# Moving the products of GpSimd to VectorE in a planned decoder kernel, with the modulation let go earlier and the planner's numbers set anew

## The chip, the cores and the metric

The kernel runs on one core of one Trainium2 chip. The metric is the device time of one launch in microseconds, as the median of several runs. A profiled execution gives the trace from which the rows below come.

## The reference, cut to what matters

A decoder trunk of two layers works on 512 tokens of width 1024, all in float32. Each layer has a mixing half and a channel half:

```python
for layer in range(DEPTH):
    mod = einsum('bd,de->be', silu(c), w_mod[layer]) + b_mod[layer]   # 6 vectors of 1024
    shift1, scale1, gate1, shift2, scale2, gate2 = split(mod, 6)
    h = rms_norm(x, mix_norm_w[layer]) * (1 + scale1) + shift1
    proj = h @ w_in[layer]                  # one product for three mixers
    y_a = deltanet_mixer(...)               # gated delta rule: conv, decay, chunks, scan
    y_b = spatial_gating_mixer(...)         # gMLP: layer norm of v, causal 128x128 mixing, gate u
    y_c = dilated_attention_mixer(...)      # three windows, merged by their denominators
    x = x + gate1 * (concat([y_a, y_b, y_c]) @ w_out[layer])
    h = rms_norm(x, ffn_norm_w[layer]) * (1 + scale2) + shift2
    gate, up = split(h @ w_ffn_in[layer], 2)
    x = x + gate2 * ((silu(gate) * up) @ w_ffn_out[layer])
```

In the gated delta rule a triangular decay matrix E is built for each chunk and masked to its causal half. In the spatial gating the mixing matrix `w_s` is masked to its causal half, and v is normalised, multiplied by `ln_g` and shifted by `ln_b`.

## The kernel before, in words

Activations lie transposed, 128 channels on the partitions and 512 tokens along the free axis. A large product is computed in three matmuls: every operand is split into a rounded part `hi` (ScalarE copies) and the rest `lo` (VectorE subtracts), and `mm3` (L581) multiplies hi by hi, hi by lo and lo by hi. One PSUM bank holds a tile of 128 by 512.

**Weights** come as pieces of 512 KB. `loader` (L454) issues their DMAs on the queue of SyncE into a ring of four `raw` buffers, in a fixed order. A buffer is free again when `splitter` (L497) has made hi and lo of it, or, for the modulation's pieces, when `modulation` (L478) has used it. `modulation` forms each of the 96 columns of `mod` with one VectorE instruction over a piece of 128 by 1024. In layer 0 the columns come in the order 0, 8, 1, 9, 2, 10, and so on: a shift, then the scale of the same chunk of 128 channels. Chunks 1 to 7 wait for the flag `go`, which the first chunk of the normalised input sets when its work has been emitted (L1463).

**The order of the work** is not written by hand. Each part of the layer is a generator, a task. `Plan` (L87) keeps estimated times of the engines, of each tile and of the DMA queue. Its `run` (L221) resumes, among the tasks that could go on, the one with the lowest priority number, and what that task emits is appended to the instruction streams of the engines. So the planner's estimates and the ranks (`PR0` for layer 0, `PR1` for layer 1) set the order in which each engine gets its instructions, and an engine runs them strictly in that order. `yield V` means: go on when VectorE's estimated queue is nearly empty. For a DMA the planner estimates the landing from a bandwidth of 423 GB/s (L177).

**The parts that the change touches.** `decay` (L801) makes one matrix E of 128 by 512 for each of four token blocks: two VectorE products with a triangle (`gts`), two matmuls with `slowr`, an exponential on ScalarE, and a product with the triangle on GpSimd (L817). `triangle` (L820) then needs E. `gmlp` (L1096) multiplies `ws` (128 by 512) by the triangle on GpSimd (L1104) and normalises v: for each of four blocks one VectorE instruction, then one GpSimd product and one GpSimd sum of 128 by 256 (L1121, L1122). Matmuls of v with `ws` follow. GpSimd also does the memsets: 24 of 64 by 512 for the attention's keys (L1219) and a few small ones.

**The tails.** At the end of a layer's projections the flag `h_done` lets the outputs of the mixers be split (`dn_out`, `gated`, `merge`), and the output projection takes them in `Y_ORDER`. `attention` (L1279) runs eight blocks for each of its two parts, at most three at a time.

Of the kernel before, what the change touches and what calls it, by code (L numbers as in the profile page):

```python
# [13 lines left out]
ALU = mybir.AluOpType  # L14
# [3 lines left out]
P = 128  # L18
T = 512
D = 1024  # L20
NB = T // P
KC = D // P
NH = 4
# [23 lines left out]
M_FIRST = 0  # L47


PR0 = dict(norm0=1, norm1=0.2, res=1.2, swin=5, val=0.2, hid=0, attn=2.5, inv=2, scan=0.4, norm=2, out=0.6, qk0=6.5,  # L50
           qk1=5, qk2=4, att0=3.5, att1=0.6, merge=2.5, gm=1.8, kd=0.1, o=1.8, tables=0.1, conv=0.2, convv=1.8, E=1,
           B=0, blocks=0.2, kss=1.2, gates=5, scales=1, tri=2.2, yb=1, qss=2.5, vv=1, split=0.2, mod=0.4)
PR1 = dict(norm0=5, norm1=2.2, res=0.1, swin=0.2, val=0.2, hid=3, attn=4, inv=1.2, scan=2.5, norm=1, out=1.2,
           qk0=2.5, qk1=4, qk2=6.5, att0=2, att1=1, merge=0.2, gm=1, kd=0.8, o=2, tables=3, conv=0.8, convv=2, E=0.1,
           B=1.5, blocks=1.8, kss=0.2, gates=6.5, scales=3.5, tri=0.1, yb=5, qss=1.8, vv=0.1, split=5, mod=0.1)
PRS = PR0, PR1
LOOSE = dict(o2=5, f1=16, t=8)
SPARE = dict(tile=1, tiles=1, n=0, out=1)
# [10 lines left out]
              qk0=[("n", i) for i in range(4)], qk1=[("n", i) for i in range(4, 8)], qk2=[("n", i) for i in range(8, 12)],  # L69
# [17 lines left out]
class Plan:  # L87
# [76 lines left out]
    def note(self, eng, op, args, kw):  # L164
        aps = [a for a in list(args) + list(kw.values()) if isinstance(a, bass.AP)]
        outs = [kw["out"] if "out" in kw else args[0]]
        if "accum_out" in kw:
            outs.append(kw["accum_out"])
        ins = [a for a in aps if not any(a is o for o in outs)]
        start = max([self.busy["Q" if eng == "D" else eng], self.now if eng == "D" else 0.0]  # L170
                    + [self.when(a, eng) for a in ins] + [self.when(o, eng) for o in outs if eng != "PE"]
                    + [self.read(o, eng) for o in outs])
        if eng == "D":
            start = max(start, self.landed[self.count % 8])
            self.busy["Q"] = start + 0.47
            scratch = any(a.space == bass.MemoryType.DRAM and "scr" in a.tensor.name for a in ins + outs)
            end = max(start + (2.2 if self.count not in (2, 3) else 3.1), self.busy["D"] + (0.9 if self.count in (2, 3) else 0)) + 4 * math.prod(outs[0].shape) / (120e3 if scratch else 423e3)  # L177
            self.busy["D"] = self.landed[self.count % 8] = end
            self.count += 1
        else:  # L180
            if eng == "S":
                self.func = args[2]
            kw = dict(kw, scalar=args[2]) if op == "scalar_tensor_tensor" else kw
            two = len([a for a in ins if a.space != PSUM]) > 1
            if eng == "V" and two and start < self.port[1] and start + 0.3 > self.port[0]:
                start = self.port[1]
            elif eng == "G" and two:
                start = max(start, min(self.busy["V"], start + 1.2))
            end = start + self.cost(eng, op, outs, ins, kw, start)
            self.busy[eng] = end  # L190
            if eng == "G" and two:
                self.port = start, end
            end += self.TAIL[eng]
        for a in ins:
            last = self.last.setdefault(a.tensor.name, {})
            last[eng] = max(last.get(eng, 0.0), end)
        for o in outs:
            name, lo, hi = self.span(o)
            w = self.wrote.setdefault(name, [])
            w[:] = [x for x in w if x[0] < lo or x[1] > hi] + [(lo, hi, end, eng)]  # L200
# [103 lines left out]
def _trunk(ctx, tc, xT, cb, consts, prm, gmp, wmod, wt, wn, wab, wo, wo2, wf1, wf2, out):  # L304
# [3 lines left out]
    PE, V, S, G, Q = plan.engines  # L308
# [41 lines left out]
    def b3(ap, n):  # L350
        return ap.rearrange("p (a b) -> p a b", a=n)
# [5 lines left out]
    def every(ap, n, w):  # L357

        return ap.rearrange("p (o j) -> p o j", o=1).to_broadcast([P, n, w])
# [28 lines left out]
    triu = cst[:, C_TRIU:C_TRIU + 128]  # L388
# [55 lines left out]
    rings, hold, go, go_lo, late = {}, [0], Flag(), Flag(), Flag()  # L444
# [33 lines left out]
    def modulation():  # L478

        soon = lambda: plan.busy["V"] - M_SLACK  # L480
        todo = [p[0] for p in pieces if p[0][0] == "mod"]
        while todo:
            _, l, j = todo.pop(0)
            near = V if l or j >= 16 else soon
            if l or j >= 16:
                mod_task.prio = PR0["mod"]
            if not l and 0 < j < 8:
                yield go
            yield near, lambda: plan.ready(raws[1][0][0]) if raws[1] and not hold[0] else None
            raw, got = raws[1].pop(0)  # L490
            bias = prs[l][:, L_BMOD + j:L_BMOD + j + 1]
            V.tensor_tensor_reduce(out=raw, in0=raw, in1=cact, op0=ALU.mult, op1=ALU.add,
                                   scale=1.0, scalar=bias, accum_out=mods[l][:, j:j + 1])
            mod_ok[l, j].done = True
            got.done = True
# [305 lines left out]
    def decay(c, g):  # L801

        yield arena.need(7)
        gts = [slot(F32R) for _ in range(2)]
        E = slot()
        for gt, gp in zip(gts, g):
            V.tensor_tensor(b3(gt, NH), every(triu, NH, P), heads(gp[:, 4 * c:4 * c + 4].bitcast(F32), NH, P), op=ALU.mult)
        yield parts_ok, tuple(gts)
        ps = yield from bank()
        PE.matmul(ps, slowr, gts[0], start=True, stop=False)  # L810
        PE.matmul(ps, slowr, gts[1], start=False, stop=True)
        free(*gts)
        yield S, ps
        S.activation(E, ps, AF.Exp)
        bankf(ps)
        yield E
        G.tensor_tensor(b3(E, NH), b3(E, NH), every(triu, NH, P), op=ALU.mult)  # L817
        return E

    def triangle(c, kT, s1, E, bc4):  # L820
# [7 lines left out]
        yield V, ps, E  # L828
        B, = yield from slots(1)
        for h in range(NH):  # L830
# [265 lines left out]
    def gmlp(l, vg):  # L1096

        ws, ln = yield from slots(2, 4)
# [2 lines left out]
        Q.dma_start(out=ln, in_=gmp[l, :, 512:1024])  # L1101
        Q.dma_start(out=bs, in_=gmp[l, :, 1024:1280])
        yield cst_ok, late, ws
        G.tensor_tensor(b3(ws, 4), b3(ws, 4), every(triu, 4, P), op=ALU.mult)  # L1104
        yield vg
        vg = vg.value
        yield V, tuple(vg)
# [9 lines left out]
        for b in range(NB):  # L1117
            yield V
            t = vg[b // 2][:, 256 * (b % 2):256 * (b % 2) + 256]
            V.tensor_scalar(t, t, mv[:, 2 * b:2 * b + 1], r[:, b:b + 1], op0=ALU.subtract, op1=ALU.mult)  # L1120
            G.tensor_tensor(t, t, ln[:, 0:256], op=ALU.mult)  # L1121
            G.tensor_tensor(t, t, ln[:, 256:512], op=ALU.add)  # L1122
        free(ln)
        yield tuple(vg)
        ts = []
        for hp in range(2):
            ps = yield from bank()
            for b in range(NB):
                for e in range(2):
# [3 lines left out]
                              start=True, stop=True)  # L1133
            yield V, ps
            t, = yield from slots(1, 4)
# [229 lines left out]
    res = lambda b: slice(b, T, 4)  # L1365
# [556 lines left out]
```

## Time and profile before

| what | value |
|---|---|
| median of 3 runs | 1485.01 us (1483.36 to 1487.52) |
| profiled execution | 1488.29 us |
| its span, first to last instruction | 1486.5 us |
| TensorE matmul busy | 1445.4 us, 97% |
| TensorE weight load busy | 1231.7 us, 83% |
| VectorE busy | 911.7 us, 61% |
| ScalarE busy | 593.0 us, 40% |
| GpSimd busy | 48.0 us, 3% |
| HBM | 119 GB/s over the span |
| mean granted TensorE clock | 0.993 |

A busy share is an average over stages: the same engine may be full in one stretch and idle in the next. Idle time in front of an engine's instruction carries the name of what ended it, as in `[2.41 <-DVE w]`: VectorE, which wrote a tile w, released it. PE is TensorE's matmul, PEld its weight load, DVE VectorE, ACT ScalarE, POOL GpSimd, SP SyncE. The program's helper (L255) records every operation, so all rows have that line, and groups are told apart by tiles and shapes.

### The profile page before, as it was taken

How to read it: one execution, taken by the hardware profiler on the slowest of the kernel's cores; microseconds unless marked ns; L12 is line 12 of the kernel's file. 1: busy time of each engine (PE TensorE's matmuls, PEld its weight loads, DVE VectorE, ACT ScalarE, POOL GpSimd, SP SyncE). 2: the span in 40 equal slices, each digit the busy share in tenths (PEclk: the TensorE clock that was granted, in tenths of full speed). 3: DMA queues.
4: the chain of work that ended last, by engine and by line, in shares of the span. 5: the costliest groups of instructions: out<-in, count | busy, mean ns of one | idle time of the engine just before them, and what ended most of it. 6: DMA issues, size and time to landing. Idle time of an engine off the chain costs nothing. (4 is left out here: it accounts for less than half of the span.)

```text
span 1486.5 us, 19674 instructions
## 1 busy us (share of the span) xinstructions
PE 1445.4 (97%) x7644; PEld 1231.7 (83%) x7644; DVE 911.7 (61%) x1870; ACT 593.0 (40%) x1048; POOL 48.0 (3%) x61
## 2 busy tenths in 40 slices
PE   7899999999999999999999899999999999999998
PEld 5687988887988888888898789988789888888887
DVE  6799996937765555555487888656476333333332
ACT  4494326564432212222346532468444222122221
POOL 0022000000000000000000300100000000000000
PEclk9999999999999999999999999999999999999999
DMA  8723462503166566656333133021141222222231
GB/s 289 248 89 105 120 208 71 164 20 116 59 214 195 187 199 196 195 187 198 93 103 94 45 105 86 29 85 36 38 156 43 99 98 90 96 99 99 99 105 52
DMA packets 70637, 178.89 MB, mean 120 GB/s; under 512 B 25104, under 2 KB 25744, under 8 KB 70544
## 3 DMA queue, kind: packets, MB, share of 16 engines
q1 hardware_dynamic: 70544, 177.64, 37.8%
q8 instruction: 60, 0.98, 0.3%
q14 instruction: 33, 0.27, 0.1%
HBM read 174.40 MB, written 3.21 MB: 119 GB/s over the span
## 5 line engine op out<-in xcount | busy, mean ns | idle before, releaser
L255 PE MATMUL b<-w,hi 128*128 128x512 f32 (+1 forms) x2748 | 844.2, 389 | 12.3 <-ACT w L255 8.6
L255 PEld LDWEIGHTS b<-w,hi 128*128 128x128 f32 x2748 | 510.8, 188 | 119.9 <-ACT w L255 11.4
L255 PE MATMUL b<-w,lo 128*128 128x512 f32 (+1 forms) x1374 | 530.6, 387 | 1.0 <-DVE lo L255 1.0
L255 ACT ACTIVATE hi<-raw 128x1024 fp32r<-128x1024 f32 (+2 forms) x215 | 222.2, 1035 | 521.0 <-PE b L255 315.8
L255 DVE TENSOR_TENSOR lo<-raw,hi 128x1024 fp32r<-128x1024 f32 (+2 forms) x215 | 256.3, 1194 | 238.4 <-ACT hi L255 237.5
L255 PEld LDWEIGHTS b<-w,lo 128*128 128x128 f32 x1374 | 258.7, 188 | 54.1 <-DVE lo L255 1.8
L255 PE MATMUL b<-w,w 128*128 128x256 f32 (+2 forms) x1808 | 219.7, 287 | 3.4 <-DVE w L255 1.6
L255 PEld LDWEIGHTS b<-w,w 128*128 128x128 f32 (+1 forms) x1808 | 204.0, 185 | 20.3 <-ACT w L255 8.6
L255 PE MATMUL b<-hi,w 128*128 128x512 f32 (+2 forms) x768 | 211.7, 363 | 0.7 <-DVE w L255 0.7
L255 ACT ACTIVATE w<-b 128x512 f32<-128x512 f32 (+1 forms) x205 | 109.2, 558 | 191.3 <-PE b L255 190.1
L255 PEld LDWEIGHTS b<-hi,w 128*128 128x128 f32 x768 | 145.4, 210 | 14.8 <-DVE w L255 1.0
L255 PE MATMUL b<-lo,w 128*128 128x512 f32 (+2 forms) x384 | 137.0, 357 | 0.0
L255 DVE CUSTOM_DVE_ANT_0 raw<-raw,cact,pr 128x1024 f32<-128x1024 f32 x96 | 122.8, 1284 | 2.4 <-DMA raw<-in_wmod_dram 2.4
L255 ACT ACTIVATE w<-w 128x512 f32<-128x512 f32 (+3 forms) x204 | 103.3, 527 | 42.1 <-DVE w L255 41.2
L255 DVE TENSOR_TENSOR w<-w,b 128x512 f32<-128x512 f32 x68 | 46.3, 686 | 109.4 <-PE b L255 108.3
L255 DVE TENSOR_TENSOR w<-w,w 128x512 fp32r<-128x512 f32 (+2 forms) x119 | 79.0, 671 | 46.8 <-ACT w L255 45.6
L255 PEld LDWEIGHTS b<-lo,w 128*128 128x128 f32 x384 | 80.4, 209 | 7.8
L255 DVE SCALAR_TENSOR_TENSOR xs<-b,mod,xs 128x512 f32<-128x512 f32 (+1 forms) x56 | 37.1, 671 | 57.1 <-PE b L255 57.0
L255 PE MATMUL b<-cst,w 128*128 128x128 f32 (+1 forms) x392 | 55.6, 273 | 3.2 <-DVE w L255 3.2
L255 PEld LDWEIGHTS b<-cst,w 128*128 128x128 f32 x392 | 46.5, 146 | 10.5 <-DVE w L255 3.8
L255 DVE SCALAR_TENSOR_TENSOR w<-w,cw,w 128x511 f32<-128x511 f32 (+2 forms) x72 | 51.9, 761 | 2.7 <-ACT w L255 2.3
L255 ACT ACTIVATE w<-w,mod 128x256 fp32r<-128x256 f32 (+1 forms) x56 | 29.8, 539 | 51.6 <-DVE w L255 51.6
(93 smaller groups left out, 659.0 us busy)
## 6 DMA issues: line engine op xcount, KB each, us to landing
raw<-in_wf_dram SPq DMA_DIRECT2D x132, 512.0 KB, 4.0
raw<-in_wmod_dram SPq DMA_DIRECT2D x96, 512.0 KB, 3.6
raw<-in_wt_dram SPq DMA_DIRECT2D x36, 512.0 KB, 3.6
raw<-in_wn_dram SPq DMA_DIRECT2D x36, 512.0 KB, 3.6
raw<-in_wo_dram SPq DMA_DIRECT2D x16, 320.0 KB, 2.9
raw<-in_wo_dram SPq DMA_DIRECT2D x6, 512.0 KB, 3.2
raw<-in_wab_dram SPq DMA_DIRECT2D x4, 544.0 KB, 5.7
xs<-in_xT_dram SPq DMA_DIRECT2D x8, 256.0 KB, 5.2
```

What stands on the lines that cost most here:

```text
L255: r = f(*args, **kw)
```

## The change

GpSimd's product of E with the triangle, its product of `ws` with the triangle, and its products and sums of the layer norm are issued on VectorE instead. The wait for `go` is left out of `modulation`. The planner estimates a DMA's landing with 350 GB/s instead of 423 from the sixteenth on. All ranks that the two tables hold may have other values. No array, no matmul and no DMA is added or left out.

```diff
-PR0 = dict(norm0=1, norm1=0.2, res=1.2, swin=5, val=0.2, hid=0, attn=2.5, inv=2, scan=0.4, norm=2, out=0.6, qk0=6.5,
-           qk1=5, qk2=4, att0=3.5, att1=0.6, merge=2.5, gm=1.8, kd=0.1, o=1.8, tables=0.1, conv=0.2, convv=1.8, E=1,
-           B=0, blocks=0.2, kss=1.2, gates=5, scales=1, tri=2.2, yb=1, qss=2.5, vv=1, split=0.2, mod=0.4)
-PR1 = dict(norm0=5, norm1=2.2, res=0.1, swin=0.2, val=0.2, hid=3, attn=4, inv=1.2, scan=2.5, norm=1, out=1.2,
-           qk0=2.5, qk1=4, qk2=6.5, att0=2, att1=1, merge=0.2, gm=1, kd=0.8, o=2, tables=3, conv=0.8, convv=2, E=0.1,
-           B=1.5, blocks=1.8, kss=0.2, gates=6.5, scales=3.5, tri=0.1, yb=5, qss=1.8, vv=0.1, split=5, mod=0.1)
+PR0 = dict(norm0=2.2, norm1=5, res=2.5, swin=2.2, val=1.2, hid=0.4, attn=2.5, inv=0.1, scan=1.8, norm=1.8, out=3.5,
+           qk0=6.5, qk1=3, qk2=4, att0=3.5, att1=0.6, merge=4, gm=2.2, kd=5, o=0.1, tables=2, conv=0.2, convv=4,
+           E=1.2, B=0, blocks=0.2, kss=1.2, gates=0.2, scales=1.5, tri=1.2, yb=4, qss=2.5, vv=6.5, split=0.2, mod=0.4)
+PR1 = dict(norm0=1, norm1=3.5, res=2, swin=3, val=0.2, hid=1, attn=4, inv=6.5, scan=2.5, norm=0.1, out=2.2, qk0=2.5,
+           qk1=3, qk2=6.5, att0=2, att1=2.2, merge=0.2, gm=4, kd=6.5, o=1.8, tables=0.2, conv=1.2, convv=2, E=0.6,
+           B=4, blocks=1.8, kss=2.5, gates=0.1, scales=0.6, tri=0.6, yb=3, qss=1.8, vv=0.1, split=2, mod=0.2)
...
-            end = max(...) + 4 * math.prod(outs[0].shape) / (120e3 if scratch else 423e3)
+            end = max(...) + 4 * math.prod(outs[0].shape) / (120e3 if scratch else 423e3 if self.count < 15 else 350e3)
...
-            if not l and 0 < j < 8:
-                yield go
...
-        yield E
-        G.tensor_tensor(b3(E, NH), b3(E, NH), every(triu, NH, P), op=ALU.mult)
+        yield V, E
+        V.tensor_tensor(b3(E, NH), b3(E, NH), every(triu, NH, P), op=ALU.mult)
...
-        G.tensor_tensor(b3(ws, 4), b3(ws, 4), every(triu, 4, P), op=ALU.mult)
+        yield V
+        V.tensor_tensor(b3(ws, 4), b3(ws, 4), every(triu, 4, P), op=ALU.mult)
...
-            G.tensor_tensor(t, t, ln[:, 0:256], op=ALU.mult)
-            G.tensor_tensor(t, t, ln[:, 256:512], op=ALU.add)
+            V.tensor_tensor(t, t, ln[:, 0:256], op=ALU.mult)
+            V.tensor_tensor(t, t, ln[:, 256:512], op=ALU.add)
```

## Rows read from the trace of the kernel before

**Rows 1.** The page, busy time: engine, busy us, share of the span, instructions.
```profile
PE 1445.4 (97%) x7644; PEld 1231.7 (83%) x7644; DVE 911.7 (61%) x1870; ACT 593.0 (40%) x1048; POOL 48.0 (3%) x61
```

**Rows 2.** Waits of TensorE: releaser, us in total, times, longest us.
```profile
PE b L255 <- DVE w L255: 17.1, 19, 2.8
```

**Rows 3.** Stretches: busy us (instructions) of each engine, granted clock, DMA share, GB/s.
```profile
15.00:20.00 5.00, 3.88 (x18) 2.62 (x17) 4.05 (x16) 2.29 (x3) 0.00 (x0) 1.00 0.59 193
...
60.00:65.00 5.00, 3.47 (x8) 2.48 (x8) 5.00 (x10) 2.07 (x3) 1.31 (x1) 0.50 0.80 279
...
105.00:110.00 5.00, 2.80 (x12) 1.96 (x14) 5.00 (x7) 4.94 (x7) 2.65 (x2) 0.72 0.37 107
...
130.00:135.00 5.00, 4.64 (x24) 4.36 (x25) 5.00 (x17) 4.50 (x15) 0.00 (x0) 0.66 0.24 90
```

**Rows 4.** GpSimd's groups: shapes, count, busy us, mean ns, idle before and releaser.
```profile
L255 POOL TENSOR_TENSOR w<-w,cst 128x512 f32<-128x512 f32 x10 | 18.0, 1816 | 519.6 <-DVE w L255 449.3 <-DMA cst<-in_consts_dram 58.6 <-ACT w L255 11.7
L255 POOL TENSOR_TENSOR w<-w,w 128x256 f32<-128x256 f32 x16 | 15.6, 992 | 105.2 <-DVE w L255 104.6
```

**Rows 5.** VectorE in order of time, layer 0: start us, us, operation, idle before.
```profile
60.10 1.75 DVE L255 SCALAR_TENSOR_TENSOR w<-w,mod,w 128x512 fp32r<-128x512 f32 x1
...
101.57 1.23 DVE L255 SCALAR_TENSOR_TENSOR w<-w,cw,w 128x511 f32<-128x511 f32 x1
...
107.07 1.21 DVE L255 SCALAR_TENSOR_TENSOR w<-w,cw,w 128x510 f32<-128x510 f32 x1
...
114.47 4.90 DVE L255 TENSOR_TENSOR w<-cst,s 128x512 fp32r<-128x512 f32 x8
...
120.63 1.07 DVE L255 TENSOR_SCALAR s<-s 128x16 int32<-128x16 int32 x1
...
124.24 1.65 DVE L255 TENSOR_SCALAR s<-s 128x16 f32<-128x16 f32 x1
125.93 0.17 DVE L255 TENSOR_TENSOR s<-s,s 128x16 f32<-128x16 f32 x1
```

**Rows 6.** VectorE in layer 1, in order of time.
```profile
828.30 8.67 DVE L255 TENSOR_TENSOR w<-cst,s 128x512 fp32r<-128x512 f32 x8
```

**Rows 7.** TensorE's instructions that waited, in order of time.
```profile
59.59 0.79 PE L255 MATMUL b<-w,hi 128*128 128x512 f32 x1 [2.73 <-ACT w L255]
61.91 0.79 PE L255 MATMUL b<-w,hi 128*128 128x512 f32 x1 [1.53 <-DVE w L255]
...
107.20 0.79 PE L255 MATMUL b<-w,band 128*128 128x512 f32 x1 [2.41 <-DVE w L255]
...
130.35 1.43 PE L255 MATMUL b<-w 128*128 128x128 f32 x8 [2.75 <-DVE w L255]
...
827.21 0.81 PE L255 MATMUL b<-s,cst 128*128 128x16 f32 x6 [1.41 <-DVE s L255]
...
835.82 0.50 PE L255 MATMUL b<-w,slowr 128*128 128x512 f32 x1 [1.11 <-DVE w L255]
```

**Rows 8.** VectorE's groups by shape: count, busy us, mean ns.
```profile
L255 DVE CUSTOM_DVE_ANT_0 raw<-raw,cact,pr 128x1024 f32<-128x1024 f32 x96 | 122.8, 1284 | 2.4 <-DMA raw<-in_wmod_dram 2.4
...
L255 DVE SCALAR_TENSOR_TENSOR w<-w,cw,w 128x509 f32<-128x509 f32 x24 | 17.7, 746 | 0.1
...
L255 DVE TENSOR_TENSOR w<-w,w 128x256 f32<-128x256 f32 x16 | 6.8, 423 | 3.0 <-ACT w L255 2.4
...
L255 DVE TENSOR_TENSOR w<-w,cst 128x512 f32<-128x512 f32 x8 | 5.5, 682 | 0.0
```

**Rows 9.** TensorE at the layers' tails, in order of time.
```profile
340.20 0.49 PE L255 MATMUL b<-w,hi 128*128 128x512 f32 x1 [1.67 <-ACT w L255]
...
1121.86 3.38 PE L255 MATMUL b<-w,w 128*128 128x256 f32 x26 [1.25 <-DVE w L255]
```

**Rows 10.** ScalarE's evictions of attention blocks that nothing else covers, layer 0.
```profile
331.76 0.60 ACT L255 ACTIVATE w<-b 128x512 f32<-128x512 f32 x1 [0.99 <-PE b L255]
...
334.64 0.60 ACT L255 ACTIVATE w<-b 128x512 f32<-128x512 f32 x1 [1.30 <-PE b L255]
```

More of the change, by code (lines that the diff above doesn't have):

```diff
@@ L176, in note @@
             scratch = any(a.space == bass.MemoryType.DRAM and "scr" in a.tensor.name for a in ins + outs)
-            end = max(start + (2.2 if self.count not in (2, 3) else 3.1), self.busy["D"] + (0.9 if self.count in (2, 3) else 0)) + 4 * math.prod(outs[0].shape) / (120e3 if scratch else 423e3)
+            end = max(start + (2.2 if self.count not in (2, 3) else 3.1), self.busy["D"] + (0.9 if self.count in (2, 3) else 0)) + 4 * math.prod(outs[0].shape) / (120e3 if scratch else 423e3 if self.count < 15 else 350e3)
             self.busy["D"] = self.landed[self.count % 8] = end
```

## The prediction, made before the changed kernel ran

> **What bounds the kernel now.** The page comes first: TensorE's matmuls are busy for 1445.4 of 1486.5 us, VectorE for 911.7 [rows 1]. So TensorE bounds the kernel, and at most 41.1 us of it are idle; what the change can win are waits of TensorE and the slow clock behind them. The list of waits comes next: VectorE's tiles ended 19 waits of TensorE, 17.1 us in all, the longest 2.8 us [rows 2]. The reader is then to see where these lie, in the stretches of 5 us [rows 3]: from 105 to 110 us TensorE works for 2.80 us of 5 while VectorE is full (5.00), and the granted clock there is 0.72; from 130 to 135 it is 0.66, from 60 to 65 it is 0.50. GpSimd is the engine that is at work just before each. Its 26 products take 18.0 and 15.6 us [rows 4], all in five places: near 60, 98 to 126, 756 and 824 to 840 us. In order of time VectorE shows what they do to it [rows 5]: an instruction on 128x16 that takes 0.17 us at 125.93 takes 1.07 at 120.63 and 1.65 at 124.24. The same eight products of the decay take 4.90 us in layer 0, where GpSimd is idle, and 8.67 us in layer 1, where it works [rows 5, 6]. TensorE's waits follow within a few us [rows 7].
>
> **The change, part by part.** Terms are made against the profiled execution, 1488.3 us, of which 1486.5 are its span; the median of the runs shown is 1485.0, 3.3 us lower, and the sum is carried over to it as a difference.
>
> *What VectorE gets.* Ten products of 128x512 at 0.68 us and sixteen operations of 128x256 at 0.42 us [rows 8]: 6.8 + 6.7 = 13.5 us, half of it in each layer.
>
> *What VectorE is freed of.* Six instructions from 101.57 to 107.07 us are about 0.5 us too long each (1.23 and 1.21 for a tap of the convolution that takes 0.75 undisturbed [rows 5, 8]): 3.0 us. Four from 120.63 to 124.24 take 1.07 to 1.65 in place of 0.17: about 4.5. One at 60.10 takes 1.75 in place of 0.75: 1.0. In layer 1 the eight decay products lose 8.67 - 4.90 = 3.8, and a few before them about as much as the six of layer 0, estimated at 3. Freed: 8.5 + 6.8 = 15.3 us, against 13.5 added. VectorE's sum hardly moves; what moves is which of its work is late.
>
> *The product with the triangle in `decay`.* Layer 0: TensorE waited 2.75 us at 130.35, and a stretch at 1.2 GHz followed [rows 7]: 0.66 is 3.4 of 5 us at half clock [rows 3], so some 1.7 us of work lost. Both gone would be 4.4. VectorE reaches the tile 4.5 - 4 x 0.68 = 1.8 us sooner, which leaves a wait of about 1 us, perhaps without the slow clock. I take 2.5; the bounds are 0 (the wait stays and only its owner changes) and 4.4. Layer 1: five waits from 827.21 to 835.82, 4.3 us in all, of which 1.41 and 1.11 are the first and the last [rows 7]. They are the decay products arriving one at a time at twice the pitch; at 4.90 us for eight, TensorE's other work between them covers most. I take 3.0. The product now stands in VectorE's queue behind what the planner put there, so the lower bound is a loss of 0.5; the upper is 4.3.
>
> *The layer norm's sixteen operations.* The wait of 2.41 us at 107.20 [rows 7] is for a small operand's rest, made on VectorE behind the six long instructions. At 0.72 over 5 us and a tail into the next, the slow clock lasted about 3.4 us, again 1.7 lost. Both together: 4.1, the upper bound. Without GpSimd the operand is ready 2 to 3 us sooner, if the eight new operations (3.4 us) come after it; if they come before, nothing is won, which is the lower bound. The operand goes first by its rank in layer 0 (`kss` 1.2, `gm` 2.2), so I take 3.0. In layer 1 the same move has no wait of its own in the rows: 0.
>
> *The product of `ws`.* At 59.65 us it held VectorE's step at 60.10 for 1.0 us, and TensorE waited 1.53 at 61.91 for that [rows 5, 7]. As a product of 0.68 us that any later place covers I take 1.0; in front of the step it would win only 0.3, and if the wait of 2.73 before it and the slow clock (0.50 for 5 us [rows 3]) shrink too, 3.5. At 756 us nothing waited: 0.
>
> *The flag.* Only the shift of chunk 1 is really held, since the flag is up when the first chunk is through. Let go, it fills idle VectorE time from 15 to 20 us (busy 4.05 of 5) and gives its `raw` buffer back about 1.3 us sooner [rows 3, 8], in a stretch where the DMAs are busy for 0.59 only. All the pieces behind it in SyncE's queue move up with it. The start is fed by DMA to 57 us, so I take 0.5. It can cost one modulation instruction, 1.3 us, if it stands before the first chunk's product, and win as much.
>
> *350 GB/s and the ranks.* Neither adds an instruction; both move the order. A later expected landing keeps instructions that need a weight from standing too early at the head of ScalarE's and VectorE's queues. The rows show what is at stake: 2.73 us at 59.59, where ScalarE's tile is late [rows 7], and 2.4 us of VectorE waiting for modulation weights [rows 8]. Value 0, bounds -2.7 and +2.4. The ranks reorder everything, the tails included, where single waits are 1 to 2 us [rows 9]. Nothing in the trace tells their sign; I take 0, with a gain or a loss of 8 us as its bounds (an estimate: a third of the 41.1 - 17.1 = 24.0 us of idle that VectorE's tiles do not end).
>
> Sum: 2.5 + 3.0 + 3.0 + 1.0 + 0.5 = 10.0 us. 1488.3 - 10.0 = 1478.3 for a profiled execution, **1475.0** for the median.
>
> A rule to weigh here. While GpSimd was in a product, VectorE's instructions were lengthened by 0.5 to 1.5 us each, and no more [rows 5]. The Trainium skill, "SBUF — State Buffer", section "SBUF: two separate sides", says that the two engines take their shared port as an exclusive lock for a whole instruction, the loser blocking fully. By that, all 33.6 us of GpSimd's products could stand in VectorE's way, and the move would free 20 us net where the rows give 1.8; the trace agrees with the blocking, not with that sum, since VectorE slips between two products.
>
> **The rivals.**
>
> *VectorE's sum decides.* TensorE's waits follow VectorE's total work in these stretches, and not single late tiles. For it: VectorE is full from 105 to 110 and from 130 to 135 us, and work moved onto a full engine has to displace some. Against it: the waits sit right behind the lengthened instructions. VectorE wins 15.3 - 13.5 = 1.8 us, and with the flag's 0.5 the time is 1482.7. The Trainium skill has a rule on this side: "Perfetto Trace Analysis", section "Optimizing Scalar/DVE Operations", holds that handing work of a saturated VectorE to GpSimd may make sense, with the caveat that both share a port. Taken without its caveat, undoing such a hand-over costs what VectorE gets.
>
> *The ranks also shorten the tails.* For it: waits at the layers' tails, such as 1.67 at 340.20 and 1.25 at 1121.86 [rows 9], end on VectorE's and ScalarE's order, which ranks set. Against it: these are chains of dependent steps. The bound's 8 us on top of the 10.0: 1467.
>
> *Slower: attention of layer 1 slides past its cover.* Its blocks run between the projections; `att1` goes from 1 to 2.2, and the weights' `split` comes from 5 to 2, in front of it, so projections run ahead and blocks are left over. Where blocks have no cover, at the end of layer 0, one is evicted each 2.9 us (331.76 to 334.64), with ScalarE waiting for TensorE's next [rows 10]. Half of that, 1.4 us, is an estimate of TensorE's loss for one. From seven blocks of sixteen on it takes back the 10.0 us; eleven cost 15.4, and the time is 1475.0 + 15.4 = 1490.4. Against it: `att0` keeps its 2, and a projection needs `hi` and `lo` of its weights in a ring of three, so it can't run far ahead.
>
> *The change does nothing on the clock* because the planner reorders around the new products so that the same tiles are late: 1485. It goes with the first rival.
>
> **How the numbers follow.** About 4.5 us (0.3%) is what a measurement can tell from no change: faster means under 1480.5, slower over 1489.5. Chances: forecast 0.47, longer tails cleared 0.18, VectorE's sum (or nothing) 0.20, slower 0.15. The forecast's own range is 1470 to 1480.5. Faster is the forecast nearly whole, the tails, and a little of the third: 0.67; same 0.18; slower 0.15. For 8 in 10 the range runs from 1463 (all upper bounds but the ranks, 4.4 + 4.3 + 4.1 + 3.5 + 1.3 = 17.6, and half of the ranks' 8) to 1489.
>
> **What would show it.** Right: no GpSimd products; the eight decay products of layer 1 near 4.9 us; instructions on 128x16 near 0.17 throughout; the waits at 107, 130 and 827 to 836 under 1 us each, and no 0.66 and 0.72 in the clock. The flag: the DMA share from 15 to 20 us over 0.59. Wrong: new waits of TensorE on VectorE of 2 us and more between 75 and 150 us, or tails after 300 and 1060 us that have grown; then the order, not the port, decided.

## The result, and the profile after

| | before | after |
|---|---|---|
| median, both kernels on one chip | 1484.7 us | 1462.1 us |
| ratio, 95% interval | | 0.9836 [0.9810, 0.9861] |
| profiled execution, and its span | 1488.29, 1486.5 us | 1461.18, 1459.0 us |

Faster by 22.6 us in the medians; the two profiled executions are 27.1 us apart. One of the six executions of the kernel after took 2404 us, at a granted clock of 0.557; the ratio, which is one of means, leaves it out.

The forecast was 1475.0 with a range from 1463 to 1489: the sign was right, the time lies just below the range, and the gain is more than twice the 10.0 us forecast.

The page of the kernel after, its busy line, answers to [rows 1]: engine, busy us, share, instructions.

```profile
PE 1437.6 (99%) x7644; PEld 1225.2 (84%) x7644; DVE 906.3 (62%) x1896; ACT 595.5 (41%) x1050; POOL 14.4 (1%) x35
```

VectorE has 26 instructions more and is busy for 5.4 us less. GpSimd's groups of the kernel after (shape, count, busy us, mean ns, idle before) answer to [rows 4]: no product is left.

```profile
L255 POOL MEMSET w<- 64x512 f32 x24 | 12.5, 521 | 976.7 <-PE b L255 960.2 <-DVE s L255 12.1 <-DVE w L255 2.3
L255 POOL MEMSET X<- 128x512 f32 x2 | 1.0, 524 | 0.0
```

TensorE's waits of the kernel after (releaser, us in total, times, longest), for [rows 2]:

```profile
PE b L255 <- ACT w L255: 11.6, 8, 6.3
PE b L255 <- DVE w L255: 2.8, 6, 1.2
PE b L255 <- DVE lo L255: 1.7, 3, 0.6
PE b L255 <- DVE s L255: 0.4, 2, 0.2
```

VectorE's tiles `w` now end 2.8 us of waits where they ended 17.1 [rows 2]. The stretches of the kernel after, with the columns of [rows 3], and two of the start for the rate of the transfers:

```profile
15.00:20.00 5.00, 3.52 (x17) 2.27 (x15) 4.65 (x17) 1.70 (x3) 0.00 (x0) 1.00 0.64 210
60.00:65.00 5.00, 4.62 (x20) 3.27 (x19) 3.71 (x11) 4.16 (x8) 0.00 (x0) 1.00 0.78 315
105.00:110.00 5.00, 5.00 (x23) 4.13 (x22) 4.83 (x10) 4.97 (x10) 0.00 (x0) 1.00 0.71 254
130.00:135.00 5.00, 5.00 (x23) 4.11 (x22) 5.00 (x8) 0.00 (x0) 0.00 (x0) 1.00 0.88 240
...
20.00:30.00 10.00, 9.28 (x40) 7.51 (x41) 8.75 (x15) 3.80 (x6) 0.00 (x0) 1.00 0.92 324
...
40.00:50.00 10.00, 9.54 (x43) 7.52 (x42) 8.21 (x13) 4.01 (x6) 0.00 (x0) 1.00 0.85 256
```

The granted clock is 1.00 in all four stretches (0.50, 0.72 and 0.66 before in the last three), and VectorE is still nearly full in the last two: a full VectorE is not what TensorE had waited for. VectorE of the kernel after in order of time, both layers, for [rows 5, 6]:

```profile
96.61 4.90 DVE L255 TENSOR_TENSOR w<-cst,s 128x512 fp32r<-128x512 f32 x8
...
106.11 1.89 DVE L255 TENSOR_TENSOR w<-w,cst 128x512 f32<-128x512 f32 x3
...
114.37 0.17 DVE L255 TENSOR_SCALAR s<-s 128x16 f32<-128x16 f32 x1
...
807.68 4.90 DVE L255 TENSOR_TENSOR w<-cst,s 128x512 fp32r<-128x512 f32 x8
```

The eight decay products take 4.90 us in both layers (8.67 in layer 1 before), the 128x16 operations 0.17. In the first row lies what the prediction did not foresee: layer 0's decay products begin at 96.61 us where they began at 114.47. TensorE's waiting instructions of the kernel after, for [rows 7, 9]; none over 0.2 us lies between 63 and 300 us or between 790 and 840:

```profile
20.73 3.94 PE L255 MATMUL b<-w,hi 128*128 128x512 f32 x16 [1.31 <-ACT w L255]
...
62.77 0.50 PE L255 MATMUL b<-w,hi 128*128 128x512 f32 x1 [0.28 <-DVE w L255]
...
367.52 0.61 PE L255 MATMUL b<-cst,w 128*128 128x1 f32 x4 [0.62 <-DVE w L255]
...
1041.58 0.49 PE L255 MATMUL b<-w,hi 128*128 128x512 f32 x1 [1.67 <-ACT w L255]
```

The wait of 1.67 us where the output projection begins is gone in layer 0 (340.20 in [rows 9]) and still there in layer 1 (1041.58).

**Where the time came from.** For every matmul, the distance from its start to the next one's is compared with the median of that distance for matmuls of the same shape. The excess holds what TensorE lost to waits and to the slow clock, and some spread besides (from 150 to 410 us the kernel after has 12.1 us of it and waits of under 2 us), so the differences count. Summed, it falls from 74.8 to 47.1 us, by as much as the span (27.5). This is one profiled execution of each; layer 1's tail (875 to 1125) varies between 16 and 19 us among the kernels with the new ranks there:

| stretch, us | lost before | lost after | gain | forecast for it |
|---|---|---|---|---|
| 0 to 75 | 19.2 | 12.5 | 6.7 | 1.5 (`ws`, flag) |
| 75 to 150 | 9.7 | 2.5 | 7.2 | 5.5 (decay, layer norm) |
| 150 to 410 | 18.2 | 12.1 | 6.1 | 0 |
| 725 to 862 | 8.7 | 4.5 | 4.2 | 3.0 (decay, layer 1) |
| 875 to 1125 | 20.0 | 16.5 | 3.5 | 0 |
| elsewhere (rounding of the medians) | -1.0 | -1.0 | 0 | 0 |

### The profile page after: what moved, and what is told of

It is laid out like the page before. It is cut to its first block, busy times and chain, and to the rows that moved or that the text cites. A ratio compares the mean times of both kernels' runs of the same rounds, so it can differ in the third digit from the quotient of the medians.

```text
span 1459.0 us, 19705 instructions
## 1 busy us (share of the span) xinstructions
PE 1437.6 (99%) x7644; PEld 1225.2 (84%) x7644; DVE 906.3 (62%) x1896; ACT 595.5 (41%) x1050; POOL 14.4 (1%) x35
## 4 chain that ended last, share of the span: by engine, by line
PE 87%; DVE 5%; ACT 3%; DMA 2%; issue 1%; SPq 0%; ACTq 0%; DVEq 0%
PE b L255 87%; DVE w L255 3%; ACT w L255 2%; DVE lo L255 1%; DMA raw<-in_wf_dram 1%; DMA raw<-in_wt_dram 1%; ACT L255 1%; DVE raw L255 1%; DVE xs L255 1%; ACT hi L255 0%; DMA cst<-in_consts_dram 0%; DVE s L255 0%; ACT s L255 0%; SPq L255 0%; DVE rt L255 0%
## 5 line engine op out<-in xcount | busy, mean ns | idle before, releaser
L255 PEld LDWEIGHTS b<-hi,w 128*128 128x128 f32 x768 | 143.7, 209 | 12.5 <-issue 0.2
L255 ACT ACTIVATE w<-w 128x512 fp32r<-128x512 f32 (+3 forms) x204 | 104.5, 528 | 45.8 <-DVE w L255 44.7
L255 DVE TENSOR_TENSOR w<-w,w 128x512 fp32r<-128x512 f32 (+2 forms) x135 | 84.9, 637 | 30.8 <-ACT w L255 29.4
L255 ACT ACTIVATE w<-w,mod 128x256 fp32r<-128x256 f32 (+1 forms) x56 | 29.8, 538 | 44.6 <-DVE w L255 44.6
```

Source lines behind the costliest of these rows:

```text
L255: r = f(*args, **kw)
```

## The experiments

Eighteen kernels, each beside the kernel before on one chip. "Layer 0" is the time to the first matmul of layer 1's first norm, "layer 1" the rest of the span, "decay" the start of layer 0's last matmul with `slowr`, all from the profiled execution, one of each kernel; the ratio has its 95% interval. How far one such execution can be off is seen in the start: after, e7, e9, r0, r1, g2, g4 and c2 have the same order of instructions on TensorE, ScalarE and VectorE up to the first matmul of 264 columns and reach it at 67.5 to 70.3 us.

| kernel | median us | ratio to before | decay | layer 0 | layer 1 |
|---|---|---|---|---|---|
| before | 1485 to 1487 | | 121.1 | 749.6 | 736.9 |
| after | 1462.1 | 0.9836 [0.9810, 0.9861] | 102.0 | 729.9 | 729.1 |
| e1 products moved, nothing else | 1520.7 | 1.0243 [1.0218, 1.0267] | 141.2 | 789.6 | 732.2 |
| e3 new ranks, nothing else | 1484.9 | 0.9989 [0.9974, 1.0005] | 114.4 | 743.5 | 739.9 |
| e4 after, products on GpSimd | 1495.6 | 1.0068 [1.0042, 1.0094] | 107.3 | 758.4 | 737.0 |
| e5 after, with the flag | 1463.6 | 0.9842 [0.9813, 0.9871] | 103.7 | 733.6 | 729.1 |
| e6 after, 423 GB/s | 1475.1 | 0.9928 [0.9902, 0.9954] | 109.0 | 745.0 | 727.6 |
| e7 after, old ranks | 1479.2 | 0.9958 [0.9940, 0.9976] | 136.6 | 749.5 | 729.0 |
| e8 old order, products on VectorE | 1482.2 | 0.9978 [0.9964, 0.9992] | 117.5 | 743.6 | 736.5 |
| e9 after, idle GpSimd products | 1476.7 | 0.9928 [0.9905, 0.9951] | 104.7 | 738.9 | 736.4 |
| r0 after, old ranks in layer 1 | 1462.6 | 0.9835 [0.9815, 0.9854] | 103.4 | 732.1 | 729.7 |
| r1 after, old ranks in layer 0 | 1481.2 | 0.9955 [0.9936, 0.9974] | 137.0 | 749.5 | 730.0 |
| g1 e1 and layer 0's gates at 0.2 | 1476.3 | 0.9929 [0.9906, 0.9953] | 109.5 | 743.1 | 730.3 |
| g2 after, gates at 3.5 | 1473.9 | 0.9927 [0.9910, 0.9944] | 117.3 | 744.1 | 727.2 |
| g3 before, gates at 0.2 | 1483.7 | 0.9983 [0.9969, 0.9997] | 113.2 | 746.6 | 736.3 |
| g4 e7 and gates at 0.2 | 1472.3 | 0.9897 [0.9877, 0.9917] | 101.7 | 740.9 | 729.3 |
| 325 after, 325 GB/s | 1475.0 | 0.9933 [0.9911, 0.9954] | 105.5 | 747.1 | 728.4 |
| 400 after, 400 GB/s | 1485.7 | 0.9994 [0.9983, 1.0004] | 106.6 | 753.8 | 731.0 |
| c1 400, merge's DMAs on GpSimd | 1484.8 | 0.9988 [0.9972, 1.0004] | 106.0 | 752.0 | 731.4 |
| c2 after, merge's DMAs on GpSimd | 1461.0 | 0.9823 [0.9804, 0.9842] | 104.2 | 731.9 | 727.3 |

Two things are to be seen. Layer 1 takes 727 to 732 us in every kernel whose planner knows the products to be VectorE's and whose GpSimd has none, whatever the ranks and the rate; in the six others (before, e3, e4, e8, e9, g3) it takes 736 to 740. Layer 0 runs from 730 to 790 us. What the change's parts do together is a matter of layer 0.

### The parts alone, and all but one

**e1, products alone.**

```diff
-        yield E
-        G.tensor_tensor(b3(E, NH), b3(E, NH), every(triu, NH, P), op=ALU.mult)
+        yield V, E
+        V.tensor_tensor(b3(E, NH), b3(E, NH), every(triu, NH, P), op=ALU.mult)
...
-            G.tensor_tensor(t, t, ln[:, 0:256], op=ALU.mult)
+            V.tensor_tensor(t, t, ln[:, 0:256], op=ALU.mult)
...
```

> The kernel before, with all of GpSimd's products issued on VectorE and nothing else of the change: the old ranks, the old 423 GB/s and the wait for the flag stay. Theory A (the port: what GpSimd's products cost VectorE is most of the gain): the waits of TensorE at 107, 130 and 827 to 836 us go, 10 to 14 us faster than before, 1471 to 1475 us. Theory B (the order: the ranks and the planner's bandwidth bring the gain, the move only fits in): under 5 us either way, 1480 to 1490 us, since without new ranks the added products stand in front of something else.

Measured: 1520.7, slower by 34.5 us, where the prediction's terms for the products say 9.5 faster. That lies outside both theories. Layer 1 gains its 5 us; layer 0 loses 40. TensorE's stretches of e1, with the columns of [rows 3], then some of its instructions in one of them:

```profile
240.00:265.00 25.00, 16.21 (x64) 13.62 (x63) 9.58 (x23) 2.36 (x10) 0.00 (x0) 0.52 0.21 63
265.00:290.00 25.00, 17.87 (x72) 15.52 (x71) 6.42 (x17) 2.35 (x10) 0.00 (x0) 0.50 0.00 1
```

```profile
250.39 2.08 PE L255 MATMUL b<-w,w 128*128 128x128 f32 x8 [0.78 <-DVE w L255]
253.32 2.07 PE L255 MATMUL b<-w,w 128*128 128x128 f32 x8 [0.85 <-DVE w L255]
```

SyncE's queue in e1, a group of issues from start to end:

```profile
245.16 79.72 SPq L255 DMA_DIRECT2D raw<-in_wmod_dram  x3
```

From 240 to 290 us only the delta rule's chain runs: mostly eight matmuls, a wait for VectorE or ScalarE, the next eight, at half clock. No projection stands between, and SyncE's queue needs 80 us to get three pieces of weights out. Its profile names the wait: 75.1 us for VectorE's `lo`, the step that empties a `raw` buffer; the `hi` in front of that `lo` stands at 315.99 us in ScalarE's order, the one before it at 237.11. Every engine is idle for a large part of the time; this is an order that ran dry, not a loaded engine.

**e3, ranks alone**, and **e7, all but the ranks**:

```diff
-PR0 = dict(norm0=1, ... gates=5, ...)
+PR0 = dict(norm0=2.2, ... gates=0.2, ...)
```

> The kernel before with the new ranks alone; GpSimd keeps its products, the planner its 423 GB/s, the modulation its wait. Theory A: 0 to 5 us faster, 1480 to 1485 us, with the waits behind GpSimd's products still there. Theory B: 10 us faster or more, 1475 us or less. That new ranks chosen for other products make it slower here (over 1490 us) fits either, and would mean that ranks and products can't be told apart by adding.

> The changed kernel with the old ranks. Theory A (the port): the move, the flag and the bandwidth keep most of it, 1463 to 1470 us. Theory B (the order): 10 us or more of the gain is lost, 1472 to 1485 us, with TensorE's waits back at the ends of the layers' projections and tails.

Measured: e3 1484.9, no change that can be told (theory A's number); e7 1479.2, 17 us slower than the whole change (theory B's). The same edit is worth nothing beside the old products and 17 us beside the new.

**e4, all but the products:**

```diff
-        V.tensor_tensor(b3(E, NH), b3(E, NH), every(triu, NH, P), op=ALU.mult)
+        G.tensor_tensor(b3(E, NH), b3(E, NH), every(triu, NH, P), op=ALU.mult)
...
```

> The changed kernel with GpSimd's products put back on GpSimd; ranks, bandwidth and flag as changed. Theory A: 10 us or more slower than the changed kernel, 1472 to 1478 us, with VectorE's instructions on 128x16 at 1 us again and TensorE's waits behind them. Theory B: within 5 us of the changed kernel, 1460 to 1467 us. In both the first 68 us stay as in the changed kernel, since only the product of ws lies there.

Measured: 1495.6, 33 us slower than the change and 10 slower than before: theory A's way, and far beyond its 1478. Some 8 us are layer 1's, the rest layer 0's; there the lost time between 150 and 410 us is 30.7 us in place of 12.1, counted as in the table of stretches. Layer 0's products are through at 112 us, so this share is one of order, not of products beside VectorE's work.

**e5, all but the flag:**

```diff
+            if not l and 0 < j < 8:
+                yield go
```

> The changed kernel with the modulation's wait for the first chunk put back. The first stage, to the first matmul of the 264 columns, ended at 74.7 us before and 68.1 us after. Theory F (the flag makes the start shorter, since buffers come back sooner): 73 to 75 us again, 5 to 7 us slower in all, 1467 to 1469 us. Theory D (the planner's 350 GB/s does, by putting the sixth chunk's scaling in front of a modulation whose weight lands late): 68 to 69 us, within 2 us of the changed kernel in all.

Measured: 1463.6; the difference of 1.5 us from the change lies within both intervals. The first stage ended at 69.4 us, near theory D's 68 to 69.

**e6, all but 350 GB/s:**

```diff
-(120e3 if scratch else 423e3 if self.count < 15 else 350e3)
+(120e3 if scratch else 423e3)
```

> The changed kernel planned with 423 GB/s throughout. Theory F: the first stage still ends at 68 us, and the time is within 3 us of the changed kernel, 1459 to 1465 us. Theory D: it ends at 73 to 75 us with a wait of TensorE of 2 us or more near 56 us and a stretch at half clock behind it, 1467 to 1470 us. As the ranks were chosen for 350, later stages can lose a few us more in either.

Measured: 1475.1, 13 us slower than the change, more than either theory had. At most 2.7 of them are there at the end of the start (the first matmul of 264 columns at 70.8 in place of 68.1 us); the lost time grows from 12.1 to 25.2 us between 150 and 410 us.

The 350 GB/s without the new ranks and without the products was not tried.

### The shared port by itself

**e8**: the order of every engine is that of before, and the products are VectorE's where GpSimd had them; the planner goes on counting them as GpSimd's.

```diff
-        G.tensor_tensor(b3(E, NH), b3(E, NH), every(triu, NH, P), op=ALU.mult)
+        nc.vector.tensor_tensor(b3(E, NH), b3(E, NH), every(triu, NH, P), op=ALU.mult)
+        plan.note("G", "tensor_tensor", ...)
```

> The kernel before, in its own order: TensorE's and ScalarE's instruction streams are the same as before, and GpSimd's products stand on VectorE at the place where they were emitted, the planner still counting them as GpSimd's. This measures the port alone, without any replanning. Theory A: VectorE is freed of about 15 us and gets 13.5, but the late tiles come sooner: 8 to 12 us faster, 1473 to 1477 us. Theory B: VectorE's sum is the same, so the waits change owner: 1482 to 1486 us.

**e9**: the order of after, and beside each moved product GpSimd does unneeded ones that nobody reads.

```diff
         V.tensor_tensor(b3(E, NH), b3(E, NH), every(triu, NH, P), op=ALU.mult)
+        for i in range(2):
+            nc.gpsimd.tensor_tensor(junk, E[:, 256 * i:256 * i + 256], E[:, 256 - 256 * i:512 - 256 * i], op=ALU.mult)
...
```

> The changed kernel, in its own order, with unneeded products on GpSimd added beside those that are on VectorE now: 20 of 128x256 beside the decay's and the mixing matrix's, 16 of 128x256 beside the layer norm's, into a tile that nobody reads; the planner doesn't see them. What it computes is the same. Theory A: VectorE's instructions beside them are lengthened by 0.5 to 1.5 us again, 10 to 15 us in all, and 6 us or more of it reach the time: 1468 us or more. Theory B: VectorE is lengthened as much, but the new order leaves room for it: under 3 us, 1461 to 1465 us.

Measured: e8 1482.2, about 3 us faster than before, as its theory B said; e9 1476.7, 14.6 slower than after, as its theory A said. In e8 two waits stay where the products now stand in front of the work that is late (TensorE of e8):

```profile
103.58 0.62 PE L255 MATMUL b<-w,band 128*128 128x512 f32 x1 [2.71 <-DVE w L255]
...
822.98 0.81 PE L255 MATMUL b<-s,cst 128*128 128x16 f32 x6 [3.26 <-DVE s L255]
```

The busy line of e9's page, its VectorE in order of time, and its TensorE:

```profile
PE 1444.5 (98%) x7644; PEld 1227.6 (83%) x7644; DVE 923.4 (63%) x1896; ACT 595.5 (40%) x1050; POOL 51.5 (3%) x71
```

```profile
109.15 3.55 DVE L255 TENSOR_TENSOR w<-w,cst 128x512 f32<-128x512 f32 x3
```

```profile
113.88 0.50 PE L255 MATMUL b<-w,band 128*128 128x512 f32 x1 [1.90 <-DVE w L255]
...
120.32 0.69 PE L255 MATMUL b<-w,w 128*64 128x128 f32 x4 [1.92 <-DVE w L255]
...
832.75 0.50 PE L255 MATMUL b<-w,band 128*128 128x512 f32 x1 [1.80 <-DVE w L255]
```

With the same 1896 instructions in the same order VectorE is busy for 17.1 us more (923.4 - 906.3) beside 51.5 - 14.4 = 37.1 us of GpSimd's products; three products with the triangle take 3.55 us in place of 1.89, and waits of 1.8 to 1.9 us are back in the same stretches. ScalarE's busy time is the 595.5 us of after, and no wait of another engine in e9 ends on a product of GpSimd, so the idle products held up nobody by their tiles. The added loss lies where they stand: 2.5 to 10.2 us from 75 to 150, 4.5 to 11.3 from 725 to 862, and under 1.5 us in any other stretch. e8 tells the same from the other side: without GpSimd's 33.6 us VectorE's busy time is 907.4, so 911.7 + 13.5 - 907.4 = 17.8 us of lengthening are gone.

In both orders the lengthening is about half of GpSimd's time. The exclusive lock of the Trainium skill's "SBUF — State Buffer" ("SBUF: two separate sides"), taken as blocking for all of that time, would make it 37 us in e9; the trace has 17.1.

GpSimd's products beside VectorE thus cost 14.6 us in the new order, with a little more GpSimd work than before had (33.6 us), and 7 of them are layer 1's (736.4 against 729.1). Taking GpSimd off and leaving the order as it was brings 3, and in layer 1 next to nothing (736.5 against 736.9).

### Which ranks, and where

**r0, r1**: the changed kernel with one of the old tables.

```diff
-PRS = PR0, PR1
+PRS = PR0, PR1_OF_BEFORE      # r0; r1: PR0_OF_BEFORE, PR1
```

> The changed kernel with the old ranks in layer 1 (layer 0 keeps the new ones). If the ranks' share of the gain comes from the decay of layer 0, whose gates are ranked 0.2 instead of 5, this keeps nearly all of it: 1462 to 1468 us, ratio 0.985 to 0.989, and the last decay matmul of layer 0 near 102 us as in the changed kernel. Rival, both layers share the 17 us that the old ranks cost: about 1470 us, ratio 0.990. If layer 1's new ranks were in fact bad, it is under 1460.

> The changed kernel with the old ranks in layer 0 (layer 1 keeps the new ones). If layer 0's decay is the place: 1474 to 1479 us, ratio 0.993 to 0.996, the last decay matmul of layer 0 after 130 us and a stretch of the delta rule's chain without cover behind it, as with all the old ranks. Rival, both layers share it: about 1470 us.

Measured: 1462.6 and 1481.2. The theory that layer 0 is the place is borne out: layer 1's new ranks are worth nothing that can be told, layer 0's carry all of it (r1 is a little slower still than was expected). That it is the decay there doesn't follow from these two.

**g1, g2, g3, g4**: one rank of the sixty-odd, on four grounds.

```diff
-           ... kss=1.2, gates=5, scales=1, ...
+           ... kss=1.2, gates=0.2, scales=1, ...      # g1 on e1, g3 on before, g4 on e7
...
-           ... kss=1.2, gates=0.2, scales=1.5, ...
+           ... kss=1.2, gates=3.5, scales=1.5, ...    # g2 on after
```

> The kernel before with the products on VectorE and one rank of 65 changed, layer 0's gates from 5 to 0.2. The products alone cost 34.5 us (1521), with the delta rule's chain running uncovered for some 65 us. Theory, the late gates are the cause: without that stretch the time falls to 1475 to 1490 us, ratio 0.993 to 1.003, and the last decay matmul of layer 0 lies before 115 us. Rival, it takes the whole new table because many ranks work together: still over 1505 us, ratio over 1.013. A half answer (1490 to 1505) says that the gates start it and other ranks hold it.

> The kernel before with one rank changed, layer 0's gates from 5 to 0.2; the products stay on GpSimd. Theory, rank and engine work together: with the gates early GpSimd's products meet more of VectorE's work, so little of the 11 us that the same rank brought with the products on VectorE (1476) is left: 1480 to 1488 us, ratio 0.997 to 1.002. Rival, the early gates alone are the gain: 1474 to 1478 us, ratio 0.993 to 0.995.

> The changed kernel with all the old ranks but one, layer 0's gates at 0.2 instead of 5. With all the old ranks it took 1479. Theory, this one rank carries the ranks' share: 1462 to 1468 us, ratio 0.985 to 0.989, the last decay matmul of layer 0 near 102 us. Rival, the share is spread over the table: 1473 to 1480 us, ratio 0.992 to 0.997.

> The changed kernel with layer 0's gates at 3.5 instead of 0.2, all else new. Theory, the gates' place is what the changed order hangs on: the last decay matmul of layer 0 moves from 102 us to over 125, and the time is 1472 to 1485 us, ratio 0.991 to 1.0. Rival, the rest of the new table pulls the decay forward by itself: the time stays within 4 us of the changed kernel, 1460 to 1466, ratio 0.983 to 0.987.

Measured: g1 1476.3, so this rank alone wins back 44 us of e1 and turns a loss of 34.5 into a gain of about 11, of which the products' move has about 8 (against g3). g3 1483.7: on GpSimd's products the same rank is worth 2 to 3 us, as the theory of rank and engine together said. g4 1472.3: between its two theories; the one rank carries 7 of the 17 us by itself, the rest takes other ranks of layer 0 beside it. g2 1473.9: the time fell where the theory put it, but the decay moved to 117.3 only, not past 125; 12 us are lost. The stretches of g1 stand against those of e1:

```profile
240.00:265.00 25.00, 25.00 (x149) 21.98 (x148) 21.19 (x70) 18.91 (x45) 2.07 (x4) 1.00 0.38 109
```

With the gates early TensorE is never idle there. Late gates alone do not make the dry stretch, though: e7 has them at 136.6 us and takes 1479. It takes them together with the order that 423 GB/s and the flag give; why that order puts the next `hi` and `lo` behind the chain was not taken apart.

### The rate of the planner

**325 and 400 GB/s** in the changed kernel:

```diff
-423e3 if self.count < 15 else 350e3
+423e3 if self.count < 15 else 325e3      # and 400e3
```

> The changed kernel planned with 325 GB/s instead of 350. In the stretches of the start the transfers ran at 250 to 325 GB/s. Theory, the nearer estimate is the gain: as good as with 350, 1459 to 1466 us, ratio 0.982 to 0.987, with no wait of TensorE over 2 us before 70 us. Rival, the ranks fit one number only and any other reshuffles: 1470 to 1480 us, ratio 0.990 to 0.997, as with 423.

> The changed kernel planned with 400 GB/s. Theory, a too early expected landing is what costs: between 350 and 423, nearer to the latter, 1466 to 1476 us, ratio 0.987 to 0.993, with a wait of TensorE of 1 to 2 us between 40 and 65 us. Rival, any other number reshuffles: no order between 325, 400 and 423, and the loss lies after 75 us rather than in the start.

Measured: 325 takes 1475.0, the rival's number, and 400 takes 1485.7, slower than either had it. With 325, 350, 400 and 423 the times are 1475, 1462, 1486, 1475, which follow no order. The theory of the nearer estimate falls (the start ran at 256 to 324 GB/s, and 325 is no better than 423); the ranks fit one number. The start is as good as with 350 (67.3 and 68.5 us where it ends). The loss is in layer 0's tail; TensorE of the kernel with 400:

```profile
350.31 1.94 PE L255 MATMUL b<-cst,w 128*128 128x128 f32 x8 [4.99 <-DVE w L255]
358.85 1.94 PE L255 MATMUL b<-cst,w 128*128 128x128 f32 x8 [6.60 <-DVE w L255]
365.51 1.52 PE L255 MATMUL b<-w,hi 128*128 128x512 f32 x2 [4.71 <-ACT w L255]
```

These are the merge of the attention and the output projection behind it. The attention's first exponential comes at 274.4 us in the changed kernel, at 284.4, 289.2 and 285.8 with 325, 400 and 423; the first VectorE step of the merge at 331.8 against 344.2, 347.8 and 342.8, when the projection has no other input left.

**c1 and c2**: is it SyncE's queue? There the merge's transfers stood behind weight pieces that waited for a buffer, its last reads from 348.38 us on with 400 GB/s.

```diff
-            Q.dma_start(out=mlscr[l][i], in_=...)
+            nc.gpsimd.dma_start(out=mlscr[l][i], in_=...)      # and the eight reads; order and planner as they were
```

> The kernel planned with 400 GB/s, with the merge's ten small transfers of each layer issued from GpSimd's queue; the order on every other engine is the same. With 400 it took 1485.7, with waits of TensorE of 4.99, 6.60 and 4.71 us between 345 and 365 us. Theory, they stood in SyncE's queue behind weight pieces (the first write from 310 to 332 us, the last reads from 340 to 348): the second part's reads start before 340 us, those three waits sum to under 6 us and the time is 1468 to 1476 us, ratio 0.988 to 0.994. Rival, the attention ends too late (its last ml at 331.6 us) and the transfers take what they take: the waits stay over 12 us together, 1482 to 1487 us.

> The changed kernel, with the merge's transfers on GpSimd's queue. Its order has the reads already at 332.3 us and no wait over 2 us there, so by the theory nothing is to be had in layer 0, and 0 to 2 us in layer 1 (1049 to 1060 us): 1459 to 1462 us, ratio 0.982 to 0.985. Rival, transfers from GpSimd start later than from SyncE: 1463 to 1468 us.

Measured: c1 1484.8, c2 1461.0. GpSimd's queue, VectorE and TensorE of c1:

```profile
340.44 2.18 POOL L344 DMA_DIRECT2D s<-mlscr  x4 [2.48 <-DMA mlscr<-ml]
```

```profile
345.38 0.82 DVE L255 TENSOR_TENSOR lo<-raw,hi 128x640 fp32r<-128x640 f32 x1 [2.57 <-ACT hi L255]
346.12 1.28 DVE L255 TENSOR_TENSOR w<-raw,w 128x512 fp32r<-128x512 f32 x2
347.33 0.17 DVE L255 TENSOR_TENSOR s<-ml,s 128x16 f32<-128x16 f32 x1
```

```profile
349.79 1.94 PE L255 MATMUL b<-cst,w 128*128 128x128 f32 x8 [4.99 <-DVE w L255]
358.32 1.94 PE L255 MATMUL b<-cst,w 128*128 128x128 f32 x8 [6.60 <-DVE w L255]
364.32 1.52 PE L255 MATMUL b<-w,hi 128*128 128x512 f32 x2 [4.06 <-ACT w L255]
```

My theory falls. The reads went out at 340.4 us, eight sooner, and nothing followed: the merge's first step (s<-ml,s) starts at 347.33 where it started at 347.85, because in VectorE's own order it stands behind the `lo` of the last output weights, and that waits for ScalarE's `hi`. The rival's numbers hold, the waits are 15.7 us together. Queue behind queue: the first one looked guilty, and a second held the same work at the same time. c2 cannot be told from the changed kernel, and none of the eighteen beats it beyond the intervals. Why the attention begins 10 to 15 us later with another rate stays open.

## Why the prediction was wrong in size and half right in cause

The time came out 12.9 us under the forecast and 0.9 under its range.

*The mechanism was right.* Its list of what would show it holds line by line: no GpSimd products, 4.90 us for the eight decay products in layer 1, 0.17 for the small operations, no wait of a microsecond at 107, 130 and 827 to 836, no 0.66 and 0.72 in the clock, a DMA share of 0.64 (0.59) from 15 to 20 us. Only the last is no sign of the flag: r0, with the same start, has 0.51 there. e9 shows the port by itself. VectorE was freed of 13.5 + 5.4 = 18.9 us, or 17.8 in the old order [e8], not 15.3.

*Decay and layer norm in layer 0* (2.5 + 3.0): 7.2 us came back between 75 and 150. In the old order [e8] it was 3: the decay's wait of 2.75 us fell to 0.71, as was forecast, but the layer norm's 2.41 stayed (2.71), because the new operations came in front of the operand; that is the case which the term's lower bound names. *Layer 1's decay* (3.0): in the old order its 4.3 us of waits became one of 3.26. In the new one layer 1 as a whole won 7.8, and 4.7 to 9.7 in every kernel that has the products moved and planned; in this profile nearly half of it is outside the waits that I had priced, in the tail, and that was left at nothing. *`ws` and flag* (1.5): the start won 6.6 us (the first matmul of 264 columns at 74.7 before, 68.1 after). With the flag back it ends at 69.4 [e5], with the products on GpSimd at 69.4 [e4], with 423 GB/s at 70.8 [e6], all within a microsecond of what kernels with the order of after show by themselves (67.5 to 70.3), so the start's gain can't be shared out among them; with the products alone moved in the old order it ends at 70.8 [e8]. The flag's price came as foreseen: the released modulation stands in front of the first chunk, whose matmuls start at 20.73 us, not 19.70 before.

*The step that failed* is "350 GB/s and the ranks": "Value 0", with bounds of -2.7 to +2.4 and of 8 us, added to the others as a term of its own. Taken out of the changed kernel they cost 13 us [e6] and 17 [e7], both beyond their bounds, and the lost time says where: from 150 to 410 us it is 12.1 us after, 25.2 with 423 GB/s and 29.8 with the old ranks. For the start alone the bounds on the rate were fair (2.7 at most); what they left out is that the number re-sorts the 300 us behind it. And the ranks are no term by themselves: nothing in the old kernel [e3], 17 us in the new.

*Under it lies an assumption that the sum never states*: that the order stays and only durations change. The products' term, 9.5 us, is about 3 in the old order [e8], -34.5 when the planner re-sorts with the old ranks [e1], about 8 with layer 0's gates early [g3 to g1], 33 with all the rest of the change [e4 to after]. In this kernel, whose order is planned, an edit's price depended on the other edits more than on its own instructions.

*The rivals.* "VectorE's sum decides" is out: VectorE is nearly full from 105 to 110 and 130 to 135 us and TensorE does not wait. "The ranks also shorten the tails", 1467, was nearest; layer 0's tail did get shorter (150 to 410 us: 6.1), but layer 1's needed no new ranks [r0]. The slower rival may have named a real mechanism in the wrong layer: in layer 0 the attention begins 10 to 15 us later with 325, 400 and 423 GB/s, the merge is late behind it, and with 400 the whole gain is lost; that the lateness is what costs there was not shown by a run of its own. One fact in the diff bore on all this and was not weighed: the gates, which feed the decay, went from rank 5 to 0.2 in layer 0, in front of the very products that were moved. The decay ended 19 us sooner than before, and 15 sooner than with the gates at 3.5 [g2].

## What to carry to other kernels

Where a planner sets the order, price an edit for its instructions, and then ask which rank or estimate lets the planner put them there; treat edits that move the same chain as one term, with bounds from the whole of the idle time and not from a third of it. To measure a shared resource apart from the order, keep the order fixed and add or take away the contender alone, as e8 and e9 do. A late transfer is worth moving only when the instruction that uses it is not itself held in its own queue.

## What the runs showed of the hardware that was not expected

In e1 TensorE was busy for 16.2 and 17.9 us of two stretches of 25 us, with waits of mostly 0.7 to 1.3 us between its groups, and the granted clock of the stretches was 0.52 and 0.50, the lower of its two levels (1.2 GHz); that kernel was at half clock for 85 us in all, the changed one for 7. From 240 to 265 us, 16.2 us of work at half clock lost 8.1, beside 8.8 us of idle time: the chain of short waits cost nearly as much again in clock as in waiting. The eight small reads landed a median 2.3 us after their issue from GpSimd's queue in c1, and 3.2 from SyncE's with 400 GB/s; the two writes the other way, 3.0 and 2.3.

Products on GpSimd lengthened VectorE's instructions beside them, single-input ones on 128x16 too (0.17 to 1.65 us [rows 5]), by about half of GpSimd's time in all (17.8 of 33.6 us, 17.1 of 37.1), and ScalarE's not.
